# Retention of a hybrid decoder trunk: q, k and g of head 1 as seven products of sums of quarters

## The chip, the core and the metric

One Trainium2 chip, one of its cores. The metric is the time of one execution on the device in microseconds, and a version's time is the median of its runs. The core has five engines with queues of their own: TensorE (PE, matmuls into PSUM), VectorE (DVE), ScalarE (ACT), GpSimd (POOL) and SyncE (SP). In this kernel SP issues the loads of the weights and POOL issues copies between DRAM buffers.

## What is computed

Two layers on 512 tokens of width 1024 in float32: retention, then a gated feed-forward with a short convolution; stick-breaking attention, then again the feed-forward; a last norm. The change lies in retention, cut here to what matters:

```python
h = _rmsnorm(x, ret_norm)                       # (512, 1024)
q, k, v, g = split(h @ w_in)                    # 4 heads: q, k 256 wide, v, g 512 wide
q, k = _rotary(q, cos, sin), _rotary(k, cos, sin) * 256 ** -0.5
scores = einsum('bhncd,bhnkd->bhnck', qc, kc) * dmat      # decay, causal
o = intra + cross                               # scores times v
o = o * lax.rsqrt(jnp.mean(o * o, axis=-1, keepdims=True) + EPS)
y = jax.nn.silu(g) * o
x = x + y @ w_out
```

## The kernel before

**Precision.** Every operand of a large product is split in two parts of type fp32r, a high part (hi, cast by ACT) and the rest (lo, subtracted by DVE). A product is three matmuls: hi with hi, lo with hi, hi with lo (`mm3`, L168 to L173). Weights come in chunks of 128 x 1024 (512 KB): SP loads a chunk into a ring of four raw tiles (L163), ACT casts it (L164), DVE subtracts (L165), into rings of four hi and four lo tiles. A raw tile is free for the next load when both casts are through, a hi or lo tile when PE has used it.

**Two ways to project.** The plain way multiplies a chunk with x (times the norm's gain, tiles xh and xl; the norm's factor r is multiplied in later): 24 matmuls of 512 columns a chunk, four chunks for a head's q and k, four for its g, four for its v. The other way (`seven`, L301) is Strassen's: weights and normalised x are cut in quarters, and seven products of sums of quarters replace eight products. Then a projection of a head is seven chunks of 24 matmuls of 256 columns. Four of the chunks are sums of weight quarters, which POOL's queue makes beforehand, by DMA from DRAM to DRAM with accumulation (`weight_sums`, L376; eight DMAs a chunk, in the order of the table `ORDER`, SP's load waits for them). The sums of normalised x, tiles xo, are made by `ret_operands` (L452): four pairs, each of some twelve DVE and four ACT instructions, used by all such projections. The products' parts are put together in SBUF by `feature_tiles` (L330: ACT copies L340, DVE adds L342).

**A head.** `ret_qk` rotates q and k (`rope`, L404: DVE L409 to L414, the split L152 on ACT and L153 on DVE, and small copies L417); `ret_v` makes the values, four blocks of tokens; `ret_scores` makes the scores (matmuls of the qk tiles) and multiplies them with the decay (L492, L485) and splits (L494, L495); `ret_av` multiplies with the values and norms (L506 to L521); `ret_y` makes the gate (L532 to L535); `out_proj_steps` projects y and adds it to x (L225), four chunks of 24 matmuls a head.

**Order.** `retention` (L538) writes the order down, and a list scheduler may move instructions a little. Heads 0 and 1 go the plain way, heads 2 and 3 by seven products (`FAST_HEAD = 2`). Before the change: q, k, v, g of head 0; q, k, then v of head 1; the first two pairs of operands beside these values; one chunk of the output projection; scores, values and gate of head 1; then the tiles of x (pool xs) are given back, the last two pairs of operands take their place (pool xb), and seven chunks of output projection stand beside them; then heads 2 and 3.

PSUM has four tiles att, three acc and one spare. On each engine instructions run in the order written, so a cast that waits for its load holds back all that stands behind it on ACT or DVE.

Of the kernel before, what the change touches and what calls it, by code (L numbers as in the profile page):

```python
# [15 lines left out]
P = 128  # L16
D = 1024
S = 512
KD = D // P
NT = S // P  # L20
EPS = 1e-6
RH, DK, DV = 4, 256, 512
# [10 lines left out]


ORDER = (
    (("fqk", 0, 1), ("fv", 0, 2), ("fg", 0, 1), ("fqk", 1, 1), ("fg", 1, 1), ("fast0_0", 0, 2), ("fast0_1", 0, 2)),
    (("fast1_0", 0, 2), ("fast1_1", 0, 2)),
)
WARM = 4
RAW = 4  # L40
FAST_HEAD = 2
FILL = (4, 2, 4, 2, 4, 2, 2, 2)


class Kernel:
# [159 lines left out]
    def out_proj(self, name, base, ys, last):  # L205
        for _ in self.out_proj_steps(name, base, ys, last):
            pass
# [209 lines left out]
            nc.scalar.copy(x, y[:, S - P :])  # L417
        return out

    def ret_qk(self, h, x):  # L420

        tail = self.sb("tl")
        tail = [tail[:, i * P : (i + 1) * P] for i in range(4)]
        own = h >= FAST_HEAD
        out = []
        for i in range(2):
            p = x[2 * i : 2 * i + 2] or [self.proj(self.wchunk("rqk", 2 * i + j), self.xs) for j in range(2)]
            out.append(self.rope(*p, self.cos, self.sin, tail[2 * i : 2 * i + 2], own))
        return *out, tail

    def ret_v(self, h):

        w = [self.wchunk("rv", 4 * h + c) for c in range(4)]
        out = []
        for i in range(NT):
            ps = self.acc()
            for k in range(KD):
                hl = [x[:, (k % 2) * S : (k % 2 + 1) * S] for x in w[k // 2]]
                xs = [x[:, i * P : (i + 1) * P] for x in self.xs[k]]
                self.mm3(ps, xs, hl, k == 0, k == KD - 1)  # L440
            rc = self.rc[:, i : i + 1]
            if i < NT - 1:
                out.append(self.split(ps, ("vv", "vv"), scale=rc))
            else:
                out.append([self.sb("vr")])
                self.nc.scalar.activation(out[i][0], ps, AF.Copy, scale=rc)
        return out

    def ret_split(self, v):
# [88 lines left out]
    def retention(self):  # L538
        nc, t = self.nc, self.t
        first = self.first4("rfirst", load=True)  # L540
        self.xpl = [self.xa, None]

        def angles(r):
            self.cos, self.sin = self.sb("tr"), self.sb("tr")
            nc.sync.dma_start(self.cos, t["cos"])
            nc.sync.dma_start(self.sin, t["sin"])
            if r is not None:
                nc.vector.tensor_mul(self.cos, self.cos, r)
                nc.vector.tensor_mul(self.sin, self.sin, r)

        def out_proj(steps, n):
            for _ in range(8 * n):
                next(steps, None)

        def out_steps(h, y, last=None):
            return self.out_proj_steps("rout", 4 * h, y, last)

        angles(self.r)
        nc.sync.dma_start(self.vec[:, 5 * KD :], t["vec"][:, 5 * KD :])
        self.rc = self.token_major_r()  # L560
        self.sums = {}
        self.weight_sums(ORDER[0], self.x[KD - 1])
        self.ops = []
        qk = self.ret_qk(0, first)
        v = self.ret_v(0)
        y = self.ret_y(0, self.ret_av(v, self.ret_scores(0, *qk)))
        qk = self.ret_qk(1, [])
        v = self.ret_v(1)
        self.ret_operands((0, 1))
        steps = out_steps(0, y)  # L570
        out_proj(steps, 1)
        y = self.ret_y(1, self.ret_av(v, self.ret_scores(1, *qk)))

        self.less_operands()
        self.more_operands("xb")
        self.xpl[1] = self.xp
        angles(None)
        out_proj(steps, 1)
        more = out_steps(1, y)
        for j in (2, 3):  # L580
            self.ret_operands((j,))
            out_proj(more, 1)
        out_proj(steps, 2)
        out_proj(more, 2)
        qk = self.ret_qk(2, self.feature_tiles("fqk", 0))
        v = [[self.sb(tag) for tag in tags] for tags in (("yy",) * NT, ("vr", "vr", "vx", "vx"))]
        self.token_rows("fv", 0, 2, S, v)
        y = self.ret_y(2, self.ret_av(self.ret_split(v[0]), self.ret_scores(2, *qk)))
        qk = self.ret_qk(3, self.feature_tiles("fqk", 1))
        steps = out_steps(2, y)  # L590
        out_proj(steps, 2)
        y = self.ret_y(3, self.ret_av(self.ret_split(v[1]), self.ret_scores(3, *qk)))
        out_proj(steps, 2)
        self.operands("xs")
        for _ in out_steps(3, y, 1):
            pass
# [323 lines left out]
def _rows(w, nk, cols):  # L920

    k, m = w.shape
    return w.reshape(nk, P, m // cols, cols).transpose(2, 1, 0, 3).reshape(m // cols, P, nk * cols)
# [17 lines left out]
def _quarters(w, nk):  # L941

    n = w.shape[1] // (4 * P)
    w = w.reshape(nk, 2, P, n, 2, 2, P)
    return w.transpose(3, 5, 1, 2, 4, 0, 6).reshape(n, 4, P, 2 * nk * P)
# [15 lines left out]
def _layout(x, ret_norm, ret_w_in, ret_w_out, sb_norm, sb_w_in, sb_w_out,  # L961
            ffn_norm, ffn_w_up, ffn_conv_w, ffn_conv_b, ffn_w_down, final_norm):
    f = np.float32
    a = {}
    a["xT"] = x[0].T.reshape(KD, P, S)
    taps = np.concatenate([ffn_conv_w, ffn_conv_b[:, None]], axis=1)
    taps = taps.reshape(2, 4, 2 * NF, P).transpose(3, 0, 2, 1).reshape(P, -1)
    norms = [_columns(v) for v in (ret_norm[0], ffn_norm[0], ffn_norm[0], sb_norm[0], ffn_norm[1], final_norm)]
    a["vec"] = np.concatenate([norms[0], norms[1], norms[3], norms[4], norms[5], taps], axis=1)
    w = ret_w_in[0]  # L970
    q, k = w[:, : RH * DK], w[:, RH * DK : 2 * RH * DK]
    v, g = w[:, 2 * RH * DK : 2 * RH * DK + RH * DV], w[:, 2 * RH * DK + RH * DV :]
    qk = np.concatenate([np.concatenate([m[:, h * DK : (h + 1) * DK] for m in (q, k)], 1) for h in range(RH)], 1)
    a["rfirst"] = qk[:, :S].reshape(KD, P, S)
    a["rqk"], a["fqk"] = _rows(qk[:, S : 2 * S], KD, P), _quarters(qk[:, 2 * S :], KD // 2)
    a["rv"], a["fv"] = _token_major(v[:, : 2 * DV]), _token_quarters(v[:, 2 * DV :])
    a["rg"], a["fg"] = _rows(g[:, : 2 * DV], KD, P), _quarters(g[:, 2 * DV :], KD // 2)
    a["rout"] = _blocks(ret_w_out[0], 4, 256)
    w = sb_w_in[0]
    q, k, v = w[:, :D], w[:, D : 2 * D], w[:, 2 * D :]  # L980
    qk = np.concatenate([np.concatenate([m[:, p * P : (p + 1) * P] for m in (q, k)], 1) for p in range(NPAIR)], 1)
    a["sfirst"] = qk[:, :S].reshape(KD, P, S)
    a["sqk"] = _rows(qk[:, S:], KD, P)
    a["sv"] = v.reshape(2, 4, P, 4, HALF).transpose(3, 0, 2, 1, 4).reshape(8, P, CH)
    w = sb_w_out[0]
    a["sout"], a["sout3"], a["sout1"] = _rows(w[:512], 4, 256), _rows(w[512:896], 3, 256), w[None, 896:]
    for l in range(2):
        g, v = ffn_w_up[l][:, :DFF], ffn_w_up[l][:, DFF:]
        first = [m[:, f * P : (f + 1) * P] for f in range(2) for m in (g, v)]
        a[f"ufirst{l}"] = np.concatenate(first, 1).reshape(KD, P, S)  # L990
        a[f"up{l}"] = _rows(np.concatenate([g[:, 2 * P :], v[:, 2 * P :]], 1), KD, P)
        for s, (lo, hi) in enumerate(STAGES[l]):
            w = ffn_w_down[l][lo * P : hi * P]
            if s < FAST[l]:
                a[f"fast{l}_{s}"] = _quarters(w, (hi - lo) // 2)
            else:
                a[f"down{l}_{s}"] = _rows(w, hi - lo, P)
    n = NF - TAIL
    w = ffn_w_down[1][TAIL * P :].reshape(n, P, n, KD // n, P)
    a["tail"] = w.transpose(2, 1, 3, 0, 4).reshape(n, P, CH)  # L1000

    freq = np.power(f(10000.0), -np.arange(0, DK, 2, dtype=f) / f(DK)).astype(f)
    ang = (freq[:, None] * np.arange(S, dtype=f)[None, :]).astype(f)
    a["cos"], a["sin"] = np.cos(ang), np.sin(ang)
    log_g = np.log(f(1.0) - np.exp2(f(-5.0) - np.arange(RH, dtype=f))).astype(f)
    diff = np.arange(-P, S, dtype=f)[None, :] - np.arange(P, dtype=f)[:, None]
    dec = np.exp(np.maximum(diff, f(0.0))[None] * log_g[:, None, None]) * f(DK**-0.5)
    a["decay"] = np.where(diff[None] >= 0, dec, f(0.0)).astype(f)
    return {n: np.ascontiguousarray(m, dtype=f) for n, m in a.items()}
# [15 lines left out]
```

## Time and profile before

| | |
|---|---|
| median of 3 runs | 1354.63 us (1354.25 to 1354.84) |
| profiled execution, its own time | 1356.42 us |
| its span, first to last instruction | 1354.6 us |
| TensorE busy | 1339.0 us (99%), 7280 matmuls |
| VectorE, ScalarE, GpSimd busy | 1035.6, 644.1, 111.7 us |
| chain that ended last | PE 94%, DVE 4% |
| moved by DMA | 217.98 MB, mean 161 GB/s |

The chain that ended last is followed back from the last instruction to whatever released each one; PE's share says how much of the span was PE's own work. A matmul's duration in the rows overlaps the next one's start, so its cost is read from starts: the distance between two, divided by the number between. "idle" in brackets is the engine's idle time before the instruction, with what ended it.

### The profile page before, as it was taken

What the parts mean: (1) busy time and instruction counts of PE and PEld (TensorE: products, weight loads), DVE (VectorE), ACT (ScalarE), POOL (GpSimd) and SP (SyncE); (2) the same over time, 40 slices, a digit from 0 to 9 for tenths busy, and PEclk for the clock granted to TensorE, in tenths of its full rate; (3) what the DMA queues carried; (4) which work ended last, traced back from release to release, by engine and by line L of the source; (5) the groups of instructions that cost most, each with busy time, mean ns of one, the idle gap of its engine ahead of it and who ended that gap; (6) DMA issues with size and microseconds to landing.
All of it is one profiled execution on the core that took longest, in us unless ns stands there. A gap on an engine that the chain in (4) does not pass through costs nothing.

```text
span 1354.6 us, 18982 instructions
## 1 busy us (share of the span) xinstructions
PE 1339.0 (99%) x7280; PEld 1152.2 (85%) x7280; DVE 1035.6 (76%) x1464; ACT 644.1 (48%) x932; POOL 111.7 (8%) x191
## 2 busy tenths in 40 slices
PE   9999999999999999999999999999999999999997
PEld 7888889899988889889988888787788899898887
DVE  7777677688769887778666578879699886787665
ACT  6544534574655444444344454445275443444434
POOL 1222221000002210000000111111000000000000
PEclk9999999999999999999999999999999999999999
DMA  9999999834349976334521664543143345235121
GB/s 328 288 286 271 276 303 299 267 105 154 102 129 280 261 207 188 108 93 126 163 78 51 189 173 118 143 115 101 39 141 107 95 139 157 85 111 173 53 70 63
DMA packets 68107, 217.98 MB, mean 161 GB/s; under 512 B 8112, under 2 KB 10288, under 8 KB 68016
## 3 DMA queue, kind: packets, MB, share of 16 engines
q1 hardware_dynamic: 45760, 146.21, 33.5%
q0 software_dynamic: 20736, 69.22, 20.6%
q8 instruction: 58, 0.95, 0.3%
q10 hardware_dynamic: 1520, 1.33, 0.3%
q14 instruction: 33, 0.27, 0.1%
HBM read 202.05 MB, written 58.72 MB: 193 GB/s over the span
## 4 chain that ended last, share of the span: by engine, by line
PE 94%; DVE 4%; issue 1%; ACT 1%; DMA 1%; DVEq 0%; ACTq 0%
PE acc L171 20%; PE acc L172 20%; PE acc L173 20%; PE x L654 6%; PE att L654 5%; PE att L171 4%; PE att L172 4%; PE att L173 4%; PE z L654 3%; PE acc L654 2%; PE att L362 2%; PE one L778 1%; PE z L750 1%; DVE sg L755 1%; PE tp L770 1%; DVE at L772 1%
## 5 line engine op out<-in xcount | busy, mean ns | idle before, releaser
L164 ACT CAST hi<-raw 128x1024 fp32r<-128x1024 f32 (+2 forms) x255 | 247.6, 972 | 352.5 <-PE acc L172 191.0
L165 DVE TENSOR_TENSOR lo<-raw,hi 128x1024 fp32r<-128x1024 f32 (+2 forms) x255 | 285.3, 1121 | 64.4 <-ACT hi L164 63.1
L172 PE MATMUL acc<-xl,hi 128*128 128x512 f32 x704 | 274.6, 390 | 0.0
L171 PE MATMUL acc<-xh,hi 128*128 128x512 f32 x704 | 274.3, 390 | 0.0
L173 PE MATMUL acc<-xh,lo 128*128 128x512 f32 x704 | 274.2, 390 | 0.0
L173 PEld LDWEIGHTS acc<-xh,lo 128*128 128x128 f32 x704 | 132.1, 188 | 27.6
L171 PEld LDWEIGHTS acc<-xh,hi 128*128 128x128 f32 x704 | 132.2, 188 | 26.8
L172 PEld LDWEIGHTS acc<-xl,hi 128*128 128x128 f32 x704 | 132.2, 188 | 26.5 <-issue 0.2
L609 DVE SCALAR_TENSOR_TENSOR tt<-tt,vec,tt 128x511 f32<-128x511 f32 (+1 forms) x176 | 131.4, 748 | 4.0 <-ACT tt L607 1.4
L606 DVE TENSOR_TENSOR tt<-acc,rr 128x512 f32<-128x512 f32 x80 | 55.1, 689 | 75.5 <-PE acc L173 75.5
L607 ACT ACTIVATE tt<-tt,vec 128x512 f32<-128x512 f32 x88 | 71.5, 812 | 11.4 <-DVE tt L606 10.3
L225 DVE TENSOR_TENSOR x<-x,acc 128x512 f32<-128x512 f32 x72 | 48.9, 685 | 35.0 <-PE acc L173 34.9
L654 PE MATMUL att<-xo,hi 128*128 128x256 f32 x384 | 70.1, 284 | 0.0
L654 PEld LDWEIGHTS att<-xo,hi 128*128 128x128 f32 x384 | 60.1, 192 | 0.2
L654 PE MATMUL att<-xo,lo 128*128 128x256 f32 x192 | 54.3, 283 | 0.0
L755 DVE TENSOR_TENSOR_SCAN sg<-sg,diag 128x512 f32<-128x512 f32 (+3 forms) x64 | 52.5, 820 | 2.2 <-ACT sg L752 1.4
L654 PE MATMUL x<-oh,hi 128*128 128x256 f32 x188 | 53.5, 284 | 0.0
L616 ACT ACTIVATE tt<-tt 128x512 f32<-128x512 f32 x44 | 27.8, 631 | 53.7 <-DVE tt L609 53.6
L654 PE MATMUL x<-oh,lo 128*128 128x256 f32 x188 | 53.2, 283 | 0.0
L654 PE MATMUL x<-ol,hi 128*128 128x256 f32 x188 | 53.2, 283 | 0.0
L173 PE MATMUL acc<-hi,xl 128*128 128x256 f32 (+1 forms) x160 | 52.0, 325 | 0.0
L172 PE MATMUL acc<-lo,xh 128*128 128x256 f32 (+1 forms) x160 | 52.0, 325 | 0.0
(556 smaller groups left out, 3056.9 us busy)
## 6 DMA issues: line engine op xcount, KB each, us to landing
raw<-in_up SPq DMA_DIRECT2D x80, 512.0 KB, 4.1
raw<-sum SPq DMA_DIRECT2D x48, 512.0 KB, 4.3
sum<-in_fast POOLq DMA_DIRECT2D x36, 512.0 KB, 9.6
sum<-sum POOLq DMA_DIRECT2D x24, 512.0 KB, 8.5
raw<-in_fast SPq DMA_DIRECT2D x18, 512.0 KB, 3.8
raw<-in_rout SPq DMA_DIRECT2D x16, 512.0 KB, 6.6
sk<-hl POOLq DMA_DIRECT2D x32, 256.0 KB, 4.1
sum<-in_fqk POOLq DMA_DIRECT2D x12, 512.0 KB, 9.2
```

What stands on the lines that cost most here:

```text
L164: nc.scalar.copy(hi, raw)
L165: nc.vector.tensor_sub(lo, raw, hi.bitcast(F32))
L171: mm(out, a[0], b[0], start=start, stop=False)
L172: mm(out, a[0], b[1], start=False, stop=False)
L173: mm(out, a[1], b[0], start=False, stop=stop)
L225: self.nc.vector.tensor_add(self.x[m], self.x[m], ps)
L606: nc.vector.tensor_mul(u, ps, self.r)
L607: nc.scalar.activation(c, u, AF.Identity, scale=w[2], bias=w[3])
L609: nc.vector.scalar_tensor_tensor(c[:, i:], u[:, : S - i], w[2 - i], c[:, i:], op0=ALU.mult, op1=ALU.add)
L616: nc.scalar.activation(g, g, AF.Silu)
L654: mm(out[:, :Q], a[ai], b[bi], start=start and k + i == 0, stop=k == nk - 1 and i == 2, skip_group_check=not start)
L755: nc.vector.tensor_tensor_scan(sg[:, :n][:, ::-1], sg[:, :n][:, ::-1], self.diag[:, S - n :][:, ::-1], 0.0, op0=ALU.mult, op1=ALU.max,)
```

## The change

Head 1's q, k and g are made by seven products too. `FAST_HEAD` goes to 1, the plain branch of `ret_qk` goes, and the weights are laid out for it: the plain q and k of head 1 (rqk) and its plain gate (rg) become quarters (fqk, fg). Each of these two gets a chunk of sums, 16 DMAs more on POOL's queue, and the table puts the sums of head 1's q, k and g first. The values of head 1 now come directly behind the gate of head 0, with the first two pairs of operands beside them; then x is given back, the last two pairs are made beside two chunks of head 0's output projection, then come q and k of head 1, one chunk, the scores, the gate, one chunk, and all of head 1's output projection. Head 1's rotation now reads SBUF tiles and angles without the norm's factor.

```diff
-    (("fqk", 0, 1), ("fv", 0, 2), ("fg", 0, 1), ("fqk", 1, 1), ("fg", 1, 1), ("fast0_0", 0, 2), ("fast0_1", 0, 2)),
+    (("fqk", 0, 1), ("fg", 0, 1), ("fqk", 1, 1), ("fv", 0, 2), ("fg", 1, 1), ("fqk", 2, 1), ("fg", 2, 1), ("fast0_0", 0, 2), ("fast0_1", 0, 2)),
...
-FAST_HEAD = 2
+FAST_HEAD = 1
...
-    def ret_qk(self, h, x):
+    def ret_qk(self, h, p):
...
-            p = x[2 * i : 2 * i + 2] or [self.proj(self.wchunk("rqk", 2 * i + j), self.xs) for j in range(2)]
-            out.append(self.rope(*p, self.cos, self.sin, tail[2 * i : 2 * i + 2], own))
+            out.append(self.rope(*p[2 * i : 2 * i + 2], self.cos, self.sin, tail[2 * i : 2 * i + 2], own))
...
-    def ret_v(self, h):
+    def ret_v(self, h, between=lambda i: None):
...
+            between(i)
...
-        qk = self.ret_qk(1, [])
-        v = self.ret_v(1)
-        self.ret_operands((0, 1))
-        steps = out_steps(0, y)
-        out_proj(steps, 1)
-        y = self.ret_y(1, self.ret_av(v, self.ret_scores(1, *qk)))
+        v = self.ret_v(1, lambda i: i < 2 and self.ret_operands((i,)))
 
         self.less_operands()
         self.more_operands("xb")
         self.xpl[1] = self.xp
         angles(None)
-        out_proj(steps, 1)
-        more = out_steps(1, y)
+        steps = out_steps(0, y)
         for j in (2, 3):
             self.ret_operands((j,))
-            out_proj(more, 1)
-        out_proj(steps, 2)
-        out_proj(more, 2)
-        qk = self.ret_qk(2, self.feature_tiles("fqk", 0))
+            out_proj(steps, 1)
+        qk = self.ret_qk(1, self.feature_tiles("fqk", 0))
+        out_proj(steps, 1)
+        y = self.ret_y(1, self.ret_av(v, self.ret_scores(1, *qk)))
+        out_proj(steps, 1)
+        for _ in out_steps(1, y):
+            pass
+        qk = self.ret_qk(2, self.feature_tiles("fqk", 1))
...
-    a["rqk"], a["fqk"] = _rows(qk[:, S : 2 * S], KD, P), _quarters(qk[:, 2 * S :], KD // 2)
+    a["fqk"] = _quarters(qk[:, S:], KD // 2)
...
-    a["rg"], a["fg"] = _rows(g[:, : 2 * DV], KD, P), _quarters(g[:, 2 * DV :], KD // 2)
+    a["rg"], a["fg"] = _rows(g[:, :DV], KD, P), _quarters(g[:, DV:], KD // 2)
```

The scheduler's order shows what stands where. On PE, ahead of the scores of head 1 (att from qk), before the change the last of a chunk of output projection (acc from yy) and then the scores block by block:

```order
L171 MATMUL acc_1292<-yy_925,hi_1273 128x512
L172 MATMUL acc_1292<-yy_926,hi_1273 128x512
L173 MATMUL acc_1292<-yy_925,lo_1274 128x512
L171 MATMUL att_1308<-qk_1002,qk_1084 128x512
L172 MATMUL att_1308<-qk_1003,qk_1084 128x512
L173 MATMUL att_1308<-qk_1002,qk_1085 128x512
L171 MATMUL att_1308<-qk_1006,qk_1088 128x512
L172 MATMUL att_1308<-qk_1007,qk_1088 128x512
L173 MATMUL att_1308<-qk_1006,qk_1089 128x512
L171 MATMUL att_1321<-qk_1002,qk_1084 128x384
```

and with the change, where L652 is a matmul of the seven products (here two of the next gate, of its fourth chunk):

```order
L173 MATMUL acc_1540<-yy_949,lo_1522 128x512
L652 MATMUL acc_1782<-xo_1016,hi_1785 128x256
L652 MATMUL acc_1782<-xo_1017,hi_1785 128x256
L171 MATMUL att_1556<-qk_1491,qk_1510 128x512
L172 MATMUL att_1556<-qk_1492,qk_1510 128x512
L171 MATMUL att_1569<-qk_1491,qk_1510 128x384
L172 MATMUL att_1569<-qk_1492,qk_1510 128x384
L171 MATMUL att_1582<-qk_1491,qk_1510 128x256
L172 MATMUL att_1582<-qk_1492,qk_1510 128x256
L483 MATMUL att_1595<-tl_1481 128x128
L173 MATMUL att_1556<-qk_1491,qk_1511 128x512
L171 MATMUL att_1556<-qk_1495,qk_1514 128x512
```

The scores moved from block by block to part by part, in the order in which the rotation gives the parts of q and k, and two matmuls of the gate moved ahead of them.

On DVE, around the end of head 1's rotation, with the change (tt_1247 to tt_1250 are the results of the seven products, lo_1720 and lo_1752 are chunks of the gate):

```order
L410 TENSOR_TENSOR tt_1483<-tt_1247,tr_1136 128x512
L165 TENSOR_TENSOR lo_1720<-raw_1718,hi_1719 128x1024
L411 TENSOR_TENSOR tt_1484<-tt_1248,tr_1136 128x512
...
L414 TENSOR_TENSOR tt_1502<-tt_1502,tt_1250 128x512
L225 TENSOR_TENSOR x_92<-x_92,acc_1526 128x512
L153 TENSOR_TENSOR qk_1511<-tt_1501,qk_1510 128x512
L225 TENSOR_TENSOR x_93<-x_93,acc_1540 128x512
L153 TENSOR_TENSOR qk_1515<-tt_1502,qk_1514 128x512
L165 TENSOR_TENSOR lo_1752<-raw_1750,hi_1751 128x1024
L492 TENSOR_TENSOR tt_1563<-att_1556,dc_1554 128x512
```

Before, the same rotation was followed by the operands and by the values' splits:

```order
L414 TENSOR_TENSOR tt_1075<-tt_1075,tt_1077 128x512
L165 TENSOR_TENSOR lo_1114<-raw_1112,hi_1113 128x1024
L153 TENSOR_TENSOR qk_1085<-tt_1074,qk_1084 128x512
L459 SCALAR_TENSOR_TENSOR tt_1232<-x_88,vec,rr_321 128x512
L153 TENSOR_TENSOR qk_1089<-tt_1075,qk_1088 128x512
L459 SCALAR_TENSOR_TENSOR tt_1233<-x_89,vec,rr_321 128x512
L156 SCALAR_TENSOR_TENSOR vv_1144<-acc_1118,rc_347,vv_1143 128x512
```

So the rotation moved from ahead of the values to just ahead of the scores, with a chunk's cast in it and one behind it.

On SP, the loads from head 1's decay on, with the change (sum is a chunk of sums):

```order
L475 DMA dc_1554<-in_decay 128x640
L163 DMA raw_1159<-in_rout 128x1024
L163 DMA raw_1213<-in_rout 128x1024
L163 DMA raw_1255<-in_fqk 128x1024
L163 DMA raw_1287<-sum_350 128x1024
L163 DMA raw_1319<-sum_351 128x1024
L163 DMA raw_1353<-in_fqk 128x1024
L163 DMA raw_1385<-sum_352 128x1024
L163 DMA raw_1417<-sum_353 128x1024
L163 DMA raw_1449<-in_fqk 128x1024
L163 DMA raw_1520<-in_rout 128x1024
L163 DMA raw_1686<-in_fg 128x1024
```

Seven chunks of q and k now stand between the output projection's, and the gate's follow one chunk later; before, head 1's decay was followed by the four chunks of its values.

## Rows read from the trace of the kernel before

**Rows 1.** The page: busy time of PE, and the chain's shares by engine.

```profile
PE 1339.0 (99%) x7280; PEld 1152.2 (85%) x7280; DVE 1035.6 (76%) x1464; ACT 644.1 (48%) x932; POOL 111.7 (8%) x191
...
PE 94%; DVE 4%; issue 1%; ACT 1%; DMA 1%; DVEq 0%; ACTq 0%
```

**Rows 2.** Windows: stretch, length; busy of PE, PEld, DVE, ACT, POOL; clock; DMA; GB/s.

```profile
83.81:105.57 21.76, 21.76 (x97) 18.02 (x96) 12.89 (x17) 6.95 (x10) 5.72 (x8) 1.00 1.02 283
206.08:226.24 20.16, 20.16 (x170) 20.15 (x169) 12.89 (x17) 9.70 (x14) 2.98 (x5) 1.00 1.05 322
```

**Rows 3.** Timeline, head 1's scores: start, us, engine, instruction, idle before it.

```profile
132.77 0.39 PE L171 MATMUL att<-qk,qk 128*128 128x512 f32 x1
...
134.41 1.05 ACT L164 CAST hi<-raw 128x1024 fp32r<-128x1024 f32 x1 [5.25 <-DMA raw<-in_rg]
...
135.50 1.23 DVE L165 TENSOR_TENSOR lo<-raw,hi 128x1024 fp32r<-128x1024 f32 x1 [1.84 <-ACT hi L164]
...
136.64 1.48 DVE L492 TENSOR_TENSOR tt<-att,dc 128x512 f32<-128x512 f32 x3
...
138.03 0.50 PE L171 MATMUL att<-p,vv 128*128 128x512 f32 x1 [1.52 <-ACT p L494]
```

**Rows 4.** Timeline of PE behind head 3's seven products of q and k.

```profile
316.06 0.40 PE L171 MATMUL acc<-yy,hi 128*128 128x512 f32 x1
...
326.97 0.39 PE L171 MATMUL att<-qk,qk 128*128 128x512 f32 x1
```

**Rows 5.** Timeline of all engines there: head 3's rotation on DVE and ACT.

```profile
314.59 1.22 DVE L165 TENSOR_TENSOR lo<-raw,hi 128x1024 fp32r<-128x1024 f32 x1
...
315.73 0.69 DVE L411 TENSOR_TENSOR tt<-tt,tr 128x512 f32<-128x512 f32 x1
...
322.50 0.62 ACT L152 CAST qk<-tt 128x512 fp32r<-128x512 f32 x1
...
324.75 0.69 DVE L153 TENSOR_TENSOR qk<-tt,qk 128x512 fp32r<-128x512 f32 x1
```

**Rows 6.** Timeline of DVE: one pair of operands, its first and last rows.

```profile
116.08 1.41 DVE L459 SCALAR_TENSOR_TENSOR tt<-x,vec,rr 128x512 f32<-128x512 f32 x2
117.40 0.75 DVE L156 SCALAR_TENSOR_TENSOR vv<-acc,rc,vv 128x512 fp32r<-128x512 f32 x1
...
120.00 1.63 DVE L469 TENSOR_TENSOR xo<-tt,xo 128x512 fp32r<-128x512 f32 x3
```

**Rows 7.** Groups of ACT at 168 to 206: casts of two pairs; busy, mean ns.

```profile
L468 ACT CAST xo<-tt 128x512 fp32r<-128x512 f32 (+1 forms) x8 | 4.4, 566 | 4.1 <-DVE tt L459 2.8 <-DVE tt L462 1.3
```

**Rows 8.** Timeline behind head 3's gate: PE's next work, last low part of y.

```profile
358.87 0.40 PE L171 MATMUL acc<-yy,hi 128*128 128x512 f32 x1
...
365.50 0.68 DVE L153 TENSOR_TENSOR qk<-tt,qk 128x512 fp32r<-128x512 f32 x1
```

**Rows 9.** Timeline of POOL: sums, first issue, first chunk's last, last of 80.

```profile
16.49 1.22 POOL L401 DMA_DIRECT2D sum<-in_fqk  x2
...
56.28 0.81 POOL L399 DMA_DIRECT2D sum<-in_fqk  x1 [5.12 <-DMA sum<-sum]
...
244.42 0.83 POOL L399 DMA_DIRECT2D sum<-in_fast  x1 [3.52 <-DMA sum<-sum]
```

**Rows 10.** The page: busy share of the DMAs in tenths, slices of 33.9 us.

```profile
DMA  9999999834349976334521664543143345235121
```

**Rows 11.** Timeline of SP's queue: a load in head 2's stretch.

```profile
214.25 0.33 SPq L163 DMA_DIRECT2D raw<-sum  x1
```

**Rows 12.** L163 alone: landing at 45:100, 100:140, 180:230, 280:330, in this order.

```profile
DMA to landing us min/median/max: 6.5/8.3/14.5
...
DMA to landing us min/median/max: 8.0/9.7/12.5
...
DMA to landing us min/median/max: 5.3/8.3/10.9
...
DMA to landing us min/median/max: 3.4/4.1/6.5
```

More of the change, by code (lines that the diff above doesn't have):

```diff
@@ L588, in retention @@
         y = self.ret_y(2, self.ret_av(self.ret_split(v[0]), self.ret_scores(2, *qk)))
-        qk = self.ret_qk(3, self.feature_tiles("fqk", 1))
+        qk = self.ret_qk(3, self.feature_tiles("fqk", 2))
         steps = out_steps(2, y)
```

## The prediction, made before the changed kernel ran

> **What bounds the kernel now.** I read the page first, then the windows of two stretches, the timeline around the scores of head 1 and after the seven products of head 3, and last the landing times of the loads. The page [rows 1] says that TensorE (PE) is busy for 1339.0 of 1354.6 us and holds 94% of the chain that ended last: nothing else is worth counting unless it makes PE wait. So the change is worth the PE time that it takes out, less the new waits that it puts into PE's order. The windows [rows 2] give the price of a matmul. Q and k of head 1 stand at 83.81 to 105.57: 96 matmuls of 512 columns in 21.76 us, 226.7 ns each. Q and k of head 2, made by seven products, stand at 206.08 to 226.24: 168 matmuls of 256 columns in 20.16 us, 120.0 ns each. The granted clock is 1.00 of 2.4 GHz in both (the counts there take in one or two neighbours cut by the edge). The timeline of head 1 [rows 3] shows the only real hole in this part of PE: 1.52 us before the product of scores and values at 138.03. Its cause is to be read upwards: a raw chunk of the gate landed late, ScalarE's (ACT) cast at 134.41 waited 5.25 us for it, VectorE (DVE) sat behind that cast with its own at 135.50, and the decay product (L492), which PE waits for, came behind both at 136.64.
>
> **What the change takes from PE.** Two projections of head 1 (q and k; g) go from 96 matmuls of 512 to 168 of 256. That is 192 x 226.7 ns = 43.5 us against 336 x 120.0 ns = 40.3 us: **3.2 us less**. The columns fall by an eighth (5.4 us of 43.5), but each matmul carries 13 ns beside its columns at 2.4 GHz, and there are 144 more. The Trainium skill (TensorE: Matmul & The Clock Gate, Back-to-back issue gap) puts an isolated gap at columns / 2.4 plus 2.5 ns; by that estimate the two would be 215.8 and 109.2 ns and the saving 4.7 us. The rows of this kernel say 3.2, and they decide.
>
> **The old hole goes: 1.5 us less.** Those gate chunks (in_rg of head 1) aren't loaded any more, and values of head 1 come 22 us earlier, far from the scores.
>
> **The new wait: 2.2 us more.** Head 1's rotation now starts when its seven products end (call that T, at 83.81 + 21.76 + 10.88 + 20.16 = 136.6 us), and behind it PE has one chunk of output projection, 24 x 226.7 ns = 5.44 us, where it had the whole of v before. The trace shows the same rotation once: head 3, where T is 316.06 and PE goes on to the scores at 326.97, 10.9 us later [rows 4]. DVE's order there is that of the change: the first half's L411 at 315.73, then sixteen operations in steps of 0.6 us to the last low part of k at 324.75 [rows 5], done at T + 9.4. The first high part of k is cast at 322.50 for 0.62 us: T + 7.1. In head 3 the 10.9 us cover this. With 5.44 us PE stands before the scores until T + 7.1, with two matmuls of the next gate (0.24 us) in between. The scores come in the order in which their parts do, the last at T + 9.8 for the first block. DVE then has one more cast of a chunk (1.14 us) in its order ahead of the decay product: L492 at 324.75 + 0.6 + 1.14, T + 10.4. In [rows 3] PE goes on 1.39 us behind L492 (136.64 to 138.03), so T + 11.8. PE's work from T to there is 5.44 + 3.74 (the scores, 132.77 to 138.03 less the hole) + 0.48 for four early gate matmuls = 9.66: 2.2 us idle. It can't be under 1.4 (the wait before the scores alone), nor over 4.9 (scores only behind the whole rotation: 9.4 + 3.74 + 1.39 - 9.66).
>
> **What keeps its cover.** Operands: by [rows 6] one pair takes DVE 116.08 to 121.63 less 0.66 for one value block, 4.9 us, so four take 19.6. From the last gate product of head 0 (about 84.4) to where PE first reads the fourth pair (117.5) there are 33 us, for these, three value blocks (2.0), four chunk casts (4.6), three operations of y and two adds (3.0): 29.2. It fits, with 3.8 to spare. The last two pairs may be written only when the last block of values has been made, at 105.6, since they take the place of normalised x; ACT's eight casts took 4.4 us [rows 7], and DVE's subtractions follow them step by step inside the 10.9 us of two chunks of projection. Gate to output projection: head 1's y has 5.44 us of cover and then its first 2.0 us of use; in head 3 [rows 8] its last low part is done at 365.50 + 0.68 with T at 358.87, so 7.3 us after, about as long: nothing added. Sums: POOL's queue issues 80 from 16.49 to 244.42 [rows 9], one in 2.9 us, so 96 end near 292. The sums of head 1's q and k, issued by 56.28, are loaded after 80; those of its gate, now second, are among the first 20, so issued near 72, and loaded from 124 on; all others come earlier in the queue than they are used by more than that. Nothing added. Six more chunk casts on ACT and DVE lie beside PE's work.
>
> **Loads behind the sums: 0.6 us more.** The DMAs are full (9 in each slice) to 271 us [rows 10]. Chunks are now eaten every 24 x 120 ns = 2.88 us where one lasted 5.44. A chunk can be loaded only when the one four before it is cast. In head 2's stretch the third chunk behind the last of q and k was issued at 214.25, 12.0 us before T [rows 11]; in the change that is the second chunk of head 1's gate, and DVE's cast of it stands in the order just ahead of L411, as in [rows 5]. To come at T - 2.9, as there, it has 9.1 us. Landing took 8.0 / 9.7 / 12.5 us (least, median, most) at 100 to 140, where head 1's seven products now stand, and 5.3 / 8.3 / 10.9 at 180 to 230 [rows 12]. I take the median of the first, 0.6 us late; the ends are 0 and 3.4. The whole rotation moves by it.
>
> **Sum.** -3.2 - 1.5 + 2.2 + 0.6 = -1.9 us. Against the profiled execution's 1356.42 us (its span of 1354.6 and 1.8 around it) that is 1354.5; the median of the runs is 1354.63, 1.8 below that execution, so the forecast is **1352.7**.
>
> **Rivals.** A measurement here can tell some 0.2%, 2.7 us.
> - *The wait is small, and the change faster*: if only the wait before the scores shows (1.4) and no load is late, -3.2 - 1.5 + 1.4 = -3.3: 1351.3. It is faster by over 2.7 as soon as both new waits are under 2.0 together. For it: landing at 180 to 230 was under 9.1 mostly. Against it: DVE's order is fixed, and the cast ahead of L492 is in it. 28%.
> - *Slower, by a late chunk*: in place of the rg chunk of today a chunk of the next gate lands late, DVE stands at its cast ahead of L411, and the rotation, the scores and PE stand behind it. Each us beyond 9.1 costs one; it decides at 9.1 + 5.2 = 14.3 us of landing (-3.2 - 1.5 + 2.2 + 5.2 = +2.7). The most at 45 to 100 us was 14.5 [rows 12], the last of four issued together: 5.4 late, 1354.63 + 2.9 = 1357.5. For it: twice the loads in the stretch with the longest landings; with no sums about (280 to 330) the median is 4.1. Against it: here the loads are paced by their casts, not issued four at a time. 15%. The Trainium skill (DMA: Bandwidth & Descriptors, Issuing engines are not separate DMA queues) says that transfers of all issuing engines run on the same 16 DMA engines and interleave; 9.7 against 4.1 agrees.
> - *Operands late*: DVE's spare 3.8 us are used up by waits on ACT, and PE stands before the seven products. At 3 us: 1355.7; it takes 4.6 to be slower. 5%.
> - *The price goes by columns alone*: if the 13 ns beside the columns were no cost of the matmul, the two projections would fall by the full eighth, 5.4 us, and the sum is -5.4 - 1.5 + 2.2 + 0.6 = -4.1: 1350.5. Against it: by [rows 2] a matmul of half the columns takes more than half, at the same clock. 2%. The Trainium skill's gap rule (TensorE: Matmul & The Clock Gate, Back-to-back issue gap) lies nearer to this than the rows do.
>
> **Numbers.** The forecast has the other 50%. Faster by over 0.2%: 28 + 2 = 30%. Within: 50 + 2 (half of the late operands) = 52%. Slower: 15 + 3 = 18%. The range runs from 1350.8 (the smallest waits, a little under 1351.3) to 1356.8: the wait and the loads both near their upper ends (-4.7 + 4.9 + 2.0 = +2.2). Its upper end leaves out the worse part of the late chunk, about one in ten.
>
> **What would show it.** Right: two stretches of 168 matmuls of 20.16 us for head 1; no hole before the seven products at 116.5; PE idle some 2 to 3 us in all between 142 and 149, before the scores (ended by ACT's cast of k) and before the values' product (ended by ACT's cast of p); L411 of the rotation near T - 0.3. Wrong: a hole at 116.5 (operands), one behind 176 (y), L411 at T + 2 or later (loads), or none at all at the scores.

## The result and the profile after

The changed kernel takes **1363.55 us** (median of 4 runs, 1362.63 to 1364.13), the kernel before 1354.45 in the same rounds: a ratio of 1.0063 with a 95% interval of 1.0050 to 1.0076, **9.1 us slower** where 1.9 us less was forecast. The profiled execution took 1363.71 us, its span 1361.8.

The page first: busy time by engine, the busy share of PE and of the DMAs in 40 slices (in tenths), and the chain's shares by engine and by line.

```profile
PE 1340.8 (98%) x7424; PEld 1159.5 (85%) x7424; DVE 1043.9 (77%) x1478; ACT 653.7 (48%) x954; POOL 123.3 (9%) x207
...
PE   9999999899999999999999999999999999999997
...
DMA  9999999984338985333522564544143345235221
...
PE 84%; DVE 6%; DMA 5%; issue 3%; ACT 2%; POOL 0%; DVEq 0%; ACTq 0%; POOLq 0%
PE acc L171 18%; PE acc L172 18%; PE acc L173 18%; PE x L652 6%; PE att L652 5%; PE att L172 3%; PE att L171 3%; PE att L173 3%; PE z L652 3%; PE acc L652 2%; DMA raw<-in_fv 2%; DMA raw<-sum 1%; DVE sg L753 1%; PE one L776 1%; DVE lo L165 1%
```

PE has 1.8 us more busy time than in [rows 1], although the change takes work from it; one slice of PE is an 8, the eighth, 238 to 272 us. The DMAs show a 9 for eight slices of 34 us, to 272 us, where [rows 10] has seven. And DMA holds 5% of the chain, 3% of it with landings of `in_fv` and `sum`, where it had 1% in all [rows 1].

Then the part that the prediction spoke of. These windows show head 1's values, its seven products of q and k, and head 1's gate (columns as in [rows 2]; the third lacks four matmuls of the gate that ran earlier and holds two of the norm).

```profile
83.03:104.79 21.76, 21.76 (x97) 18.02 (x96) 21.56 (x40) 11.82 (x17) 6.22 (x9) 1.00 1.04 268
115.67:135.82 20.15, 20.15 (x169) 20.15 (x168) 12.55 (x16) 9.64 (x14) 5.59 (x9) 1.00 1.04 329
155.35:175.97 20.62, 20.57 (x170) 20.26 (x169) 16.33 (x20) 12.85 (x18) 5.44 (x8) 1.00 1.03 303
```

No hole stands before the seven products at 115.67, and none behind the gate. The timeline of PE around head 1's scores has three waits, 2.0 us in all:

```profile
142.41 0.50 PE L652 MATMUL acc<-xo,hi 128*128 128x256 f32 x2 [0.95 <-ACT hi L164]
143.32 0.50 PE L171 MATMUL att<-qk,qk 128*128 128x512 f32 x1 [0.41 <-ACT qk L152]
148.06 0.96 PE L171 MATMUL att<-p,vv 128*128 128x512 f32 x3 [0.63 <-ACT p L494]
```

So far all is as forecast. PE reaches head 2's scores at 262.29, 2.05 us earlier than before (264.34). There the time goes. The timeline of PE at head 2's scores:

```profile
262.29 0.50 PE L171 MATMUL att<-qk,qk 128*128 128x512 f32 x1 [0.51 <-DVE yy L373]
268.53 0.56 PE L171 MATMUL att<-qk,qk 128*128 128x256 f32 x1 [3.53 <-ACT vr L371]
272.33 0.79 PE L171 MATMUL att<-p,vv 128*128 128x512 f32 x1 [1.32 <-ACT p L494]
```

What released PE is L371 on ScalarE, which empties the last value blocks and so frees an `att` buffer for the third block of scores. The timeline of ACT shows what stood in front of it:

```profile
259.32 1.06 ACT L164 CAST hi<-raw 128x1024 fp32r<-128x1024 f32 x1 [2.45 <-DMA raw<-in_fg]
263.12 1.05 ACT L164 CAST hi<-raw 128x1024 fp32r<-128x1024 f32 x1 [2.74 <-DMA raw<-sum]
264.07 0.62 ACT L152 CAST vv<-yy 128x512 fp32r<-128x512 f32 x1
266.93 1.05 ACT L164 CAST hi<-raw 128x1024 fp32r<-128x1024 f32 x1 [2.25 <-DMA raw<-sum]
267.88 1.08 ACT L371 ACTIVATE vr<-att 128x512 f32<-128x512 f32 x2
270.71 1.05 ACT L164 CAST hi<-raw 128x1024 fp32r<-128x1024 f32 x1 [1.75 <-DMA raw<-in_fg]
271.66 0.62 ACT L494 CAST p<-tt 128x512 fp32r<-128x512 f32 x1
```

Four chunks of head 2's gate, which PE needs, but for two early products, only from 283 us on, come late one after another, and each time ACT stands at the cast: L371 is behind the third, the scores' own cast (L494) behind the fourth. VectorE does the same with the low parts (L165 at 268.01 and 271.79, ahead of L492 and L495). The landing times of SP's loads issued at 247 to 262 us, changed kernel first, then the kernel before, same stretch:

```profile
DMA to landing us min/median/max: 11.2/11.5/12.5
```

```profile
DMA to landing us min/median/max: 4.1/4.6/5.7
```

Why 11.5 and not 4.6 is to be seen on POOL's queue. The sums of fast0_1, which ended at 244.42 [rows 9], now end here:

```profile
289.73 0.85 POOL L399 DMA_DIRECT2D sum<-in_fast  x1 [2.00 <-DMA sum<-sum]
```

The last part is the clock. The windows around the wait (the eighth column is the granted clock):

```profile
258.00:268.50 10.50, 6.49 (x29) 4.94 (x27) 4.86 (x7) 4.19 (x6) 1.91 (x3) 1.00 1.06 275
268.50:279.00 10.50, 9.03 (x30) 7.77 (x31) 5.06 (x9) 2.87 (x6) 1.65 (x2) 0.51 1.04 370
279.00:289.00 10.00, 10.00 (x75) 9.69 (x74) 5.80 (x8) 8.98 (x15) 1.94 (x3) 1.00 0.88 194
```

Behind the wait of 3.53 us the clock is at 1.2 GHz for about 10 us. From the first score to the gate the same matmuls took 11.04 us before; now they take 20.72 us, of which PE is idle for 4.96 and busy for 15.76: 4.7 us are the slower clock. With the 0.51 in front that is 10.2 us lost, less what was won ahead of it.

### The profile page after: what moved, and what is told of

Its sections match the earlier page's. It is cut to its first block, busy times and chain, and to the rows that moved or that the text cites. A ratio compares the mean times of both kernels' runs of the same rounds, so it can differ in the third digit from the quotient of the medians.

```text
span 1361.8 us, 19327 instructions
## 1 busy us (share of the span) xinstructions
PE 1340.8 (98%) x7424; PEld 1159.5 (85%) x7424; DVE 1043.9 (77%) x1478; ACT 653.7 (48%) x954; POOL 123.3 (9%) x207
## 4 chain that ended last, share of the span: by engine, by line
PE 84%; DVE 6%; DMA 5%; issue 3%; ACT 2%; POOL 0%; DVEq 0%; ACTq 0%; POOLq 0%
PE acc L171 18%; PE acc L172 18%; PE acc L173 18%; PE x L652 6%; PE att L652 5%; PE att L172 3%; PE att L171 3%; PE att L173 3%; PE z L652 3%; PE acc L652 2%; DMA raw<-in_fv 2%; DMA raw<-sum 1%; DVE sg L753 1%; PE one L776 1%; DVE lo L165 1%
## 5 line engine op out<-in xcount | busy, mean ns | idle before, releaser
L164 ACT CAST hi<-raw 128x1024 fp32r<-128x1024 f32 (+2 forms) x261 | 255.5, 979 | 360.1 <-PE acc L172 184.1
L165 DVE TENSOR_TENSOR lo<-raw,hi 128x1024 fp32r<-128x1024 f32 (+2 forms) x261 | 294.2, 1130 | 75.6 <-ACT hi L164 74.9
L172 PE MATMUL acc<-xl,hi 128*128 128x512 f32 x666 | 259.7, 390 | 0.0
L171 PE MATMUL acc<-xh,hi 128*128 128x512 f32 x666 | 259.6, 390 | 0.0
L173 PE MATMUL acc<-xh,lo 128*128 128x512 f32 x666 | 259.5, 390 | 0.0
L173 PEld LDWEIGHTS acc<-xh,lo 128*128 128x128 f32 x666 | 125.0, 188 | 26.2
L652 PE MATMUL att<-xo,hi 128*128 128x256 f32 x576 | 105.2, 284 | 0.0
L652 PEld LDWEIGHTS att<-xo,hi 128*128 128x128 f32 x576 | 89.9, 191 | 0.3
L652 PE MATMUL att<-xo,lo 128*128 128x256 f32 x288 | 81.5, 283 | 0.0
L225 DVE TENSOR_TENSOR x<-x,acc 128x512 f32<-128x512 f32 x72 | 48.9, 686 | 33.7 <-PE acc L173 33.6
L652 PE MATMUL x<-oh,hi 128*128 128x256 f32 x196 | 55.7, 284 | 0.0
L652 PE MATMUL x<-ol,hi 128*128 128x256 f32 x196 | 55.5, 283 | 0.0
L652 PE MATMUL x<-oh,lo 128*128 128x256 f32 x196 | 55.5, 283 | 0.0
L652 PEld LDWEIGHTS att<-xo,lo 128*128 128x128 f32 x288 | 54.9, 191 | 0.1
## 6 DMA issues: line engine op xcount, KB each, us to landing
sum<-in_fast POOLq DMA_DIRECT2D x36, 512.0 KB, 10.2
```

The lines of the kernel that those rows point to most:

```text
L164: nc.scalar.copy(hi, raw)
L165: nc.vector.tensor_sub(lo, raw, hi.bitcast(F32))
L171: mm(out, a[0], b[0], start=start, stop=False)
L172: mm(out, a[0], b[1], start=False, stop=False)
L173: mm(out, a[1], b[0], start=False, stop=stop)
L225: self.nc.vector.tensor_add(self.x[m], self.x[m], ps)
```

## The experiments

Theory 1: the longer queue of sums makes SP's loads land late just where the casts of four chunks stand ahead of head 2's scores. Rival A: SP's own larger demand, or the order that the change makes, does it whatever POOL does.

**e1: the sums of fast0 later.** Only POOL's order differs from the changed kernel; that of PE, ACT, DVE and SP is the same throughout.

```diff
-    (..., ("fg", 2, 1), ("fast0_0", 0, 2), ("fast0_1", 0, 2)),
-    (("fast1_0", 0, 2), ("fast1_1", 0, 2)),
+    (..., ("fg", 2, 1)),
+    (("fast0_0", 0, 2), ("fast0_1", 0, 2), ("fast1_0", 0, 2), ("fast1_1", 0, 2)),
```

> The changed kernel, with the sums of both fast0 weights moved from the front of the program to the list that is issued at the start of the first feed-forward; the order on TensorE, ScalarE, VectorE and SyncE is the same as in the changed kernel, only POOL's differs. Theory 1 (POOL's sums, which now run to 289.7 us, make the chunks of head 2's gate land 11 to 12.5 us after issue instead of 4 to 6, and their casts then stand in front of head 2's scores): the four chunks land within 4 to 6.5 us, the hole of 3.53 us before the second block of att<-p and the 10 us at a granted clock of 0.5 are gone, the stretch from head 2's first score matmul to the gate takes 11 to 12.5 us instead of 20.7, and the time is 1363.5 less 8.5 to 10 = 1353.5 to 1355. Rival A (the order of the casts itself, or SyncE's own larger demand, makes the hole, whatever POOL does): landing 9 us or more, hole and low clock stay, 1362.5 to 1364. Rival B (the fall of the clock is not of the hole's making but of the order of matmuls there): hole gone, but 4 us or more of low clock stay, 1357 to 1359.

Measured: 1354.2 us, ratio to before 0.9995 (0.9986 to 1.0004). Landing of the loads issued at 247 to 262 us:

```profile
DMA to landing us min/median/max: 3.2/4.3/4.3
```

PE waits for nothing between 225 and 290 us, and the clock is 1.00, here in the window that had 0.51:

```profile
268.50:279.00 10.50, 10.50 (x80) 10.19 (x79) 5.86 (x9) 9.40 (x16) 0.00 (x0) 1.00 0.11 30
```

Rivals A and B fall: with the order of all other engines unchanged, the 9 us are gone when POOL's sums are moved.

**e2: only fast0_1 later** (that entry alone moved to the second list).

> The changed kernel with only the second half of these sums (fast0_1, 16 DMAs) moved later, so that POOL's queue holds fast0_0 last, as many bytes less as the change had added and some more. Theory 1: POOL's queue ends near 250 us, some us before the gate's chunks land; the last two or three of them land within 7 us, the hole is under 1 us, no low clock, 1353.5 to 1356. Rival A: as the changed kernel, 1362.5 to 1364. If only the first chunk is still late: a hole of 1 to 2 us and about 1355 to 1358.

Measured: 1353.6 us, 0.9993 (0.9984 to 1.0002); POOL's last sum at 241.13, no wait at head 2's scores.

**e7: half of fast0_1 later** (`("fast0_1", 0, 1)` in the first list, `("fast0_1", 1, 1)` in the second).

> The changed kernel with one half of fast0_1's sums (8 of its 16 DMAs) moved later: between e2 (POOL's last sum at 241.1 us, no hole) and the changed kernel (289.7 us, 10 us lost). Theory 1 (what counts is whether sums are still in flight while the gate's chunks, issued at 248 to 258 us, are on their way): POOL's last sum near 265 us, the first two or three chunks of the gate land 8 to 12 us after issue, the fourth earlier; the hole is 1 to 4 us, with or without a low clock: 1356 to 1362. Rival (the loss needs all of the bytes, as a total of the stretch and not at that place): less than 1.5 us lost, 1353.5 to 1355.

Measured: 1357.65 us, 1.0026 (1.0016 to 1.0036). Landing in the same stretch, and PE's longest waits from 84 to 330 us:

```profile
DMA to landing us min/median/max: 4.4/8.2/11.8
```

```profile
PE att L171 <- ACT p L494: 1.4, 2, 0.8
PE att L362 <- DVE vx L373: 1.4, 1, 1.4
```

Between the two, as theory 1 has it, though POOL's last sum came at 277.32, not near 265. The waits are split up (the longest is 1.4 us) and the clock stays at 1.00; it costs some 4 us more than e2, not 10.

**e3: more sums in the kernel before.** The projections stay as they were.

```diff
-    (..., ("fg", 1, 1), ("fast0_0", 0, 2), ("fast0_1", 0, 2)),
-    (("fast1_0", 0, 2), ("fast1_1", 0, 2)),
+    (..., ("fg", 1, 1), ("fast1_0", 0, 2), ("fast0_0", 0, 2), ("fast0_1", 0, 2)),
+    (("fast1_1", 0, 2),),
```

> The kernel before, with 16 more sum DMAs (fast1_0) put on POOL's queue ahead of the fast0 ones, nothing else changed: projections, evacuations and the order of the four other engines as before. Theory 1: POOL's queue ends near 290 us instead of 244.4, the chunks of head 2's gate (issued 250 to 258) land 9 to 12 us after issue instead of 4 to 6, the hole of head 2's scores appears, with or without a low clock: plus 3 to 10 us, 1357.5 to 1364.5. Rival A (SyncE's extra chunks of the changed projections, or the order the change makes, are needed as well): landing stays under 7 us or the casts have room, 1354 to 1355.5.

Measured: 1364.08 us, 1.0062 (1.0050 to 1.0075), the loss of the changed kernel without its change. PE's waits from 225 to 290 us, the landing, and the window with the low clock:

```profile
PE att L171 <- ACT vr L371: 4.4, 1, 4.4
PE att L171 <- DVE yy L373: 0.2, 1, 0.2
```

```profile
DMA to landing us min/median/max: 11.5/12.3/13.7
```

```profile
268.50:279.00 10.50, 7.66 (x30) 6.50 (x31) 5.75 (x10) 4.52 (x8) 1.66 (x2) 0.67 1.02 336
```

**e4: the sums of fast0 later in the kernel before**, the control.

> The kernel before with both fast0 sums moved later: the control for what moving them costs or gives in itself. Theory 1: head 2's loads already landed in 4 to 6 us, so nothing to gain there: 1353 to 1355. If the sums at 400 us stand in the way of loads there: 1355 to 1357.

Measured: 1355.24 us, 1.0002 (0.9993 to 1.0010): moving the sums is worth nothing in itself. The median is 0.24 above the interval given, within the spread of the runs.

**e6: late chunks, but their casts behind the scores.** All sums stay at the front. Theory 2: lateness costs only through what stands behind the late cast.

```diff
+        self.held -= 1
+        if 0 <= self.held < 3:
+            with self.tc.issue_after(self.last_p):
+                nc.scalar.copy(hi, raw)
+        else:
+            nc.scalar.copy(hi, raw)
```

(`last_p` is the last cast of the scores; `held` is set to 4 ahead of head 2's gate, so that the second to fourth chunk are held.)

> The changed kernel with all its sums where they are, so that the chunks still land late; only the casts on ScalarE of the second to fourth chunk of head 2's gate are queued behind the last cast of head 2's scores, instead of in front of the evacuation of the last value blocks. Theory 2 (the late chunks cost time because their casts stand in front of the work of the scores on ScalarE and VectorE, and the clock falls because of that hole): landing stays at 9 us or more after issue, the hole of 3.53 us and the 1.32 us behind it fall under 1 us in sum, no low clock, the gate's chunks are cast while the values' products run: 1354 to 1357. Rival (the chunks are late whatever stands behind them: TensorE then waits at the gate's second or third product instead): 3 us or more of waits in the gate from about 274 us on, 1358 to 1363.

Measured: 1355.06 us, 1.0000 (0.9992 to 1.0009). The landing, PE's waits from 225 to 290 us (line numbers up to 9 higher), and the window:

```profile
DMA to landing us min/median/max: 10.2/11.5/12.7
```

```profile
PE att L368 <- DVE lo L171: 0.9, 2, 0.5
PE att L177 <- DVE yy L379: 0.5, 1, 0.5
PE att L368 <- DVE vx L379: 0.4, 1, 0.4
```

```profile
268.50:279.00 10.50, 10.50 (x73) 9.98 (x73) 8.85 (x14) 9.97 (x17) 1.32 (x2) 1.00 1.03 370
```

The chunks land as late as in the changed kernel (11.5 us), the DMAs are as full, and 8.5 us are back. The scheduler moved more than the three casts: the same chunks' low parts on DVE and two early gate matmuls on PE went behind with them, so what was tried is the place of the late chunks' whole use. So it takes both: late chunks, and an order in which their casts stand in front of urgent work.

**e5: a cover for head 1's rotation**, on e2.

```diff
-        out_proj(steps, 1)
+        out_proj(steps, 2)
         y = self.ret_y(1, ...)
-        out_proj(steps, 1)
+        qk = self.ret_qk(2, self.feature_tiles("fqk", 1))
         for _ in out_steps(1, y):
             pass
-        qk = self.ret_qk(2, self.feature_tiles("fqk", 1))
```

(and y of head 1 in tiles `yy`, since `qk` now holds head 2's.)

> The kernel of e2 (only fast0_1's sums moved later), with two edits against the wait at head 1's scores: both chunks of head 0's output projection that are left stand between head 1's rotation and its scores (before: one there and one behind y), and head 2's q and k by seven products stand ahead of head 1's output projection, as the cover of head 1's y and with that projection as the cover of head 2's rotation. Theory 1 (the 2.0 us of waits at 142 to 148 us come from a cover of 5.6 us on TensorE for a rotation of 9.9 us on VectorE): with 11 us of cover these waits fall under 0.5 us and nothing new opens: 1353.6 less 1.0 to 2.0 = 1351.6 to 1352.6. Rival A (the new order of the loads or of the casts opens a hole elsewhere, at head 2's scores or at head 1's y): waits move, 1353 to 1356. Rival B (the waits are of the scores' own chain, not of the rotation): 1353.3 to 1354.2.

Measured: 1355.9 us, 1.0006 (0.9998 to 1.0015). Theory 1's half on head 1 is right, no wait is left there; but rival A came true, with one wait and a low clock in the window behind it:

```profile
209.92 0.50 PE L171 MATMUL acc<-yy,hi 128*128 128x512 f32 x1 [2.44 <-DVE x L225]
```

```profile
203.00:210.00 7.00, 4.57 (x21) 3.46 (x19) 7.00 (x13) 4.88 (x11) 1.68 (x2) 1.00 1.06 337
210.00:217.00 7.00, 7.00 (x24) 5.57 (x25) 6.09 (x8) 1.28 (x2) 2.16 (x3) 0.76 1.06 209
```

DVE did nearly all of head 2's rotation, needed 50 us later, before the first L225, which frees the accumulator that PE waits for.

**e8: the same with the rotation written behind the projection.**

```diff
-        qk = self.ret_qk(2, self.feature_tiles("fqk", 1))
+        tiles = self.feature_tiles("fqk", 1)
         for _ in out_steps(1, y):
             pass
+        qk = self.ret_qk(2, tiles)
```

> The kernel of e5 with head 2's rotation written behind head 1's output projection instead of ahead of it, so that on VectorE the first evacuations of that projection stand in front of most of the rotation. e5's profile shows one wait of 2.44 us (acc waited for the evacuation into x, which stood behind the rotation) and 3.4 us at a granted clock of 0.5 behind it. Theory 1 (that order on VectorE is the whole of e5's loss, as the order of the casts was at head 2's scores): no wait over 0.5 us between 84 and 330 us, no low clock, 1355.9 less 2.4 and some 1.7 = about 1351.8 where the kernel before shows 1355. Rival (waits move to head 2's rotation or to the value products): a wait of 1 us or more remains, 1353 to 1355.

Measured: **1351.14 us**, ratio to before 0.9975 (0.9966 to 0.9984). This window from head 1's values to head 3's scores holds no wait:

```profile
84.00:330.00 246.00, 245.95 (x1528) 223.40 (x1527) 194.02 (x275) 136.75 (x216) 37.28 (x54) 1.00 0.85 260
```

**e9: e8's order and e6's casts, all sums at the front.**

> The same cover for head 1's scores and the same place of head 2's rotation as in e8, but with all sums at the front of the program as in the changed kernel, and the casts of head 2's gate behind its scores as in e6. Theory 2 (lateness costs nothing where no cast of a late chunk stands in front of work that TensorE waits for): landing 9 us or more, waits under 1.5 us in sum between 84 and 330 us, no low clock, 1351.5 to 1353.5. Rival (with loads this late, a product waits for its chunk somewhere once the order ahead of it is tighter): waits of 2 us or more, perhaps a low clock, 1354 to 1360.

Measured: 1351.77 us, 0.9978 (0.9969 to 0.9987); one wait of 0.4 us in the same stretch. Landing:

```profile
DMA to landing us min/median/max: 9.2/10.3/11.4
```

Theory 2 stands: loads more than twice as late as in the kernel before, and 3.4 us faster than it. e8 and e9 are both faster than either kernel; their intervals don't tell them apart.

**r_before and r_after: both kernels again, unchanged.**

> The kernel before, unchanged, for a second profile: e3 and e4, which are the same program up to about 150 us, show 0.99 and 0.86 us of wait at head 1's scores where the first profile of the kernel before had 1.52. If the first was an outlier (theory 1): about 0.9, and a span near 1353. If the wait is 1.5 as a rule: 1.4 to 1.6.

> The changed kernel, unchanged, on the chip and in the rounds of this call: 1362.5 to 1364.5, with a wait of 3 to 5 us before the third block of head 2's scores and a granted clock of 0.5 for some us behind it. If wait and clock were those of one execution (rival): a wait under 2 us, or a clock of 1.00 throughout.

Measured: r_before has a span of 1353.8 us and this wait at head 1's scores, little more than a third of that in [rows 3]:

```profile
136.12 0.97 PE L171 MATMUL att<-p,vv 128*128 128x512 f32 x3 [0.57 <-ACT p L494]
```

r_after: 1363.11 us, 1.0057 (1.0040 to 1.0073), with 4.3 us of wait for L371, 1.9 for L494, and a clock of 0.67 in the window of 268.5 to 279. The loss is no accident of one execution.

## Why the prediction was wrong

The time from head 0's first score matmul to head 3's, by the timelines, shows the own effect of the change free of how each execution started, and of all that follows. PE's waits within it stand beside it.

| kernel | head 0 to head 3, us | waits of PE, us |
|---|---|---|
| before, first profile | 276.67 | 1.5 |
| r_before | 275.67 | 0.6 |
| e4 (before, sums later) | 276.01 | 0.9 |
| after | 285.07 | 7.5 |
| e1 (after, sums later) | 274.89 | 2.1 |
| e2 (after, fast0_1 later) | 274.18 | 1.7 |
| e8 | 271.76 | 0.1 |

- **Price of the matmuls, 3.2 less: right.** The stretches take 20.15 and 20.6 us, where 20.16 were expected from [rows 2], and e8, which has hardly a wait, needs 276.01 - 271.76 = 4.25 us less than e4, 3.4 without their waits. In the order of the changed kernel less of it is left: reckoned in the same way, e1 and e2 need 2.4 and 2.6 less than e4. The Trainium skill's isolated gap (TensorE: Matmul & The Clock Gate, Back-to-back issue gap), by which it would have been an estimated 4.7, doesn't agree with the 226.7 and 120.0 ns of the rows.
- **The old hole, 1.5 less: too large.** It was the first profile's. Three other profiles, of r_before, e4 and e3, which are one program up to there, have 0.57, 0.86 and 0.99: some 0.8. The forecast took a term from an execution 1.8 us above the median and set it against the median.
- **The new wait at head 1's scores, 2.2: right, as the sum of three.** 0.95 + 0.41 + 0.63 = 2.0; the first falls on one of the early gate products, whose chunk ACT cast from 141.31 to 142.36, not on the scores as forecast. L492, behind L225 twice and one chunk cast (L165) on DVE, ran at T + 10.8 where 10.4 was said (T is the end of the seven products of q and k, 135.82); the late load of the next point is the difference. e5 and e8 take it away with 11 us of cover.
- **Late loads ahead of head 1's rotation, 0.6: 0.4, and it is part of those 2.0.** L411 came at 135.91 with T at 135.82, 0.1 after T, where head 3 had it 0.3 before. So the two terms came to 2.0 of idle time where 2.8 was forecast. The forecast reckoned from starts, and so reckoned they are 2.6: from T to the values' product at 148.06 it took 12.24 us, for which the forecast had 9.66 of work. The idle time leaves out that the last matmul before a wait lasts longer in the rows (0.39 us) than the step from one start to the next (0.23).
- **Operands and y keep their cover: right.** No wait at 115.67 nor at 176.
- **"Sums: ... Nothing added": the step that failed.** It asked of the sums only whether each is made before it is loaded, and gave no term to what they do to other loads; at head 2 the runs showed 10.2 us for that. That POOL's queue would end near 292 us was worked out rightly (289.73). In the kernel before, head 2's gate chunks were issued 5.5 to 13.5 us behind the last sum, and landed in 4.6 us for that reason. The 16 further sums took this lull away; e3 shows that it needs nothing else of the change. The rows read for the forecast passed over the place: [rows 10] was read as full to 271 us, though its nines end at 237, and none of the four stretches of [rows 12] lies between 230 and 280 us.
- **"Slower, by a late chunk", 15%: the mechanism, in the wrong place and at the wrong price.** It was put at head 1, where one cast stood in the way, with a microsecond lost for each one beyond 9.1 of landing, so that it decided at 14.3. At head 2 four casts stand in ACT's and DVE's order ahead of L371, L494 and the decay products, and the landing was only 11.5. There ACT's four waits for chunks alone are 9.2 us. And behind the wait of 3.5 us another 4.7 us went to the lower clock.

The rule cited there (DMA: Bandwidth & Descriptors of the Trainium skill, Issuing engines are not separate DMA queues) was the right one, and the trace agrees: 11.5 us of landing with sums about, at a DMA share of 1.04 to 1.06, and 4.3 without (e1). It was weighed only where the change stood.

What stays open: the last 1 to 2 us. With the late loads out of the way the change, forecast at 1.9 less, is worth this much: e1 is 1.1 us ahead of e4 at head 3, e2 1.8; at the end it is 1.0 and 1.6 by the medians, which a measurement here can't tell from nothing. That the low clock comes of the wait was not tried by itself: no profile holds so long a wait at a full clock. e5's twelve executions only hint at it: three with a mean granted clock of 0.998 or 0.999 took 1353.70 to 1354.55 us, the nine with 0.996 or 0.997 took 1355.66 to 1358.39, but only one, of the nine, has a trace.

## What to carry to other kernels

When a change makes a background queue longer, look at what is issued between its old end and its new one: loads that landed quickly there did so in the lull behind it. A late load costs what stands behind its cast in the engines' order; so where an order is set ahead of time, put casts of chunks that aren't needed yet behind the work that TensorE waits for (e6 won 8.5 us with every load still late). Take the size of an old wait from more than one profile before booking it as a gain.

## What the runs showed that was not expected

TensorE's granted clock fell to 0.5 (1.2 GHz) around the end of a wait in four profiles, between 1.1 us before the end (e3) and 1.4 us behind it (e5): at a wait of 3.53 us in the changed kernel (clock low for 10.2 us, with a second wait of 1.32 in it), 4.34 in r_after (6.8), 4.38 in e3 (6.8) and 2.44 in e5 (3.4). In all other profiles, whose longest wait in this part was 1.52 us, it stayed at 1.00 there. So such a wait cost nearly twice its length: in e5 a single one of 2.44 us cost 4.4 us up to head 3 (276.12 against e8's 271.76), where the program as written differs in nothing but the place of the rotation; in the changed kernel 5.5 us of waits at head 2's scores cost 10.2. In e7 the waits from 257 to 270 us came to 3.2 us, none over 1.4, and the clock stayed at 1.00.
